# Down projection with its first two token pairs interleaved, part stores one block later, and row sums spread over blocks

## The chip, the cores and the metric

The kernel runs on one core of a Trainium2 chip. The metric is the device time of one launch in microseconds: before the change 2499.06 us, the median of three runs (2497.41 to 2502.0). The engines are named as in the profile: PE is TensorE (the matrix engine), PEld its weight loads, DVE VectorE, ACT ScalarE, POOL GpSimd, SP SyncE, which here only issues transfers.

## What is computed

One layer of a hybrid encoder for 17 tiles of 128 tokens (2048 tokens of a prompt, 8 x 16 of running streams), width 1024, hidden width 2816. Two mixers (a gated delta rule and a short gated convolution) come first; the change doesn't touch them. Then follows the feed-forward part:

```python
    mix = jnp.concatenate([o, sc_out.astype(x.dtype)], axis=-1) @ w_o
    x = x + rmsnorm(mix, norm_mix_post)

    h = rmsnorm(x, norm_ffn_pre)
    f = (jax.nn.silu(h @ w_gate) * (h @ w_up)) @ w_down
    x = x + rmsnorm(f, norm_ffn_post)
    return x, conv_new, S_new, sc_new
```

All is float32. The matrix engine gets each operand as two fp32r parts, a rounded one (made by a cast on ACT) and what the rounding left (made by a subtraction on DVE or POOL), and every product is three matmuls: high by high, high by low, low by high.

## The kernel before

**Blocks.** The large products of the feed-forward part are done by a scheme with seven products on 2x2 blocks instead of eight. Both operands are needed in seven combinations of blocks ("parts"), and the results are put together from the seven products.

**Gate and up** (`gate_up`, 1095 to 2018 us). Tokens go in three passes `gi` over groups of 6, 6 and 5 tiles; in each pass 22 blocks `f` of 128 hidden columns are done. A block is 84 matmuls (L1284) of 128x384, or 128x320 in the last pass: four products into four banks (`gu_start`), then three more onto three of these. Between the two, ACT copies the first sums out of the banks (`m1`, `m7`, `m5`, L1316 to L1318), and the later matmuls overwrite these banks. DVE combines the copies with the later sums, and ACT applies the SiLU (L1327, L1332). The product of gate and up is the hidden activation; DVE makes the activation parts for the down projection from it (tile `pt`, written in every other block), and the DMA queue of ACT stores them (`partd` L1356 and L1358, `lastd` L1350 for the fifth tile of the odd group). The stores stand at the end of the block in the text; they wait for DVE's sums in `pt`.

The first operand of the next pass is prepared while a pass runs: `hs` are loaded after blocks 4 to 11, and at block 16 (`f == NF - 6`) `ffn_sums` makes all row sums of that operand, three DVE operations for each of four `k`, twelve in one go (L1182 to L1185).

**Down** (`down_pair`, `down_single`, `down_chunk`, 2018 to 2485 us). The hidden width is cut into five chunks `ch` of 4, 4, 4, 4 and 6 blocks (`FCHUNKS`), so `c` is 2 in the first four and 3 in the last. In each chunk all pairs of token tiles are gone through: eight pairs and a `single`. A pair has seven products, each of `c` x 3 matmuls of 128x512 (L1450), from 7 activation parts and 7 x `c` weight parts. Activation parts are loaded from `partd` (`load_parts`, tile `ar`, three buffers) and split (`split`, L1431 ACT cast, L1434 subtraction on DVE or POOL). A weight part is made from raw weights (`dr`, four buffers) by a cast on ACT (L1132) and a subtraction on POOL, each third one on DVE (L1134); `prep_step` does one such step. A ring of `NDW` = 21 weight parts lies in four `dr`, one `sA`/`sB`, twelve `da` and four `dn` tiles. The sums leave the banks by DVE additions (L1409) into `acc`, or in chunk 0 by ACT copies. `fbank` hands out the eight PSUM banks in turn; a pair takes four.

In chunk 0 the first two activation parts of the first pair (`first_parts`) and five weight parts are made during pass 2 of gate and up (`f` = 4 and 11 to 15).

**The end of a pair.** In the last chunk `finish` squares the sum (ACT, L1459), makes the norm's factor (L1460, L141, POOL L143), multiplies with the gain (DVE L1463), adds the residual (DVE L1468) and stores both halves of the result, one by ACT's queue and one by SP's (L1470). `down_pair` ends with two more DVE subtractions there (L1509, L1510). The `single` comes last in the last chunk (`tail`), after the first pair in the others.

**What sets the order.** Each engine executes its instructions in order. That order comes from a scheduler that simulates the engines over the text of the kernel (`issue_after` gives it edges); the text's order is its priority. DMA issues stand in the order of the engine that issues them, so a transfer that waits for data holds back all later transfers of its queue.

Of the kernel before, what the change touches and what calls it, by code (L numbers as in the profile page):

```python
# [86 lines left out]
def kernel(  # L87
# [1010 lines left out]
    SUMS = ("sA", "sB", "sC", "sD")  # L1098

    def down_chunk(ch):  # L1100
# [11 lines left out]
        def part(i, q):  # L1112
# [12 lines left out]
            if m == NDR:  # L1125
                w = [ks.tile([P, 512], F32R, tag=nm, name=nm) for nm in SUMS[:2]]
            else:
                pool, b = (dr, NDR) if m < NDR else (da, NDQ) if m <= NDR + NDQ else (dn, NDW - NDR - 1 - NDQ)
                w = pool.tile([P, 2, 512], F32R, tag="dw", name="dw", bufs=b)
                w = [w[:, 0], w[:, 1]]  # L1130
# [30 lines left out]
    with ExitStack() as ph:  # L1161
# [14 lines left out]
        def ffn_sums(gi, hs, fs):  # L1176
            hw = len(FGROUPS[gi]) * P // 2
            t3, t2 = [], []
            for k in range(KH):
# [8 lines left out]
        def ffn_prep(gi, hs, sums=None, fs=None):  # L1188
# [3 lines left out]
            for nm in PARTS:  # L1192
                for k in range(KH):
                    b11, b12, b21, b22 = blocks(gi, hs, k)
                    if nm == "T3" and not sums:
                        t3.append(fs.tile([P, HW], F32, tag="t3", name="ft3", bufs=KH)[:, :hw])
# [36 lines left out]
        def gu_weights(gi, f):  # L1233
# [12 lines left out]
            else:  # L1246
                nc.sync.dma_start(out=rg, in_=w_gu[f, 0].rearrange("p k c -> p (k c)"))
                wl[:] = [nc.sync.dma_start(out=ru, in_=w_gu[f, 1].rearrange("p k c -> p (k c)"))]
                s = [(fe if q > 1 else ks).tile([P, 512], F32R, tag=nm, name=nm).bitcast(F32) for q, nm in enumerate(SUMS)]
# [55 lines left out]
        def gate_up(gi, f, X, banks):  # L1305
# [12 lines left out]
            A.copy(s5, b4)  # L1318
# [27 lines left out]
            if n % 2:  # L1346
                for vi, v in enumerate((v1, v2)):
                    nc.scalar.dma_start(out=lastd[ch][:, kk % 2, q, vi * 64:vi * 64 + 64], in_=v[:, hw - 64:hw])
            if kk % 2:
# [5 lines left out]
                for j in range(n // 2):  # L1355
                    nc.scalar.dma_start(out=partd[gi][ch][j, :, 1:7, q, :], in_=pt[:, :, j * P:(j + 1) * P])  # L1356
            else:
                nc.scalar.dma_start(out=partd[gi][ch][:, :, 0, q, :].rearrange("j p c -> p j c"),  # L1358
                                    in_=v1[:, :n // 2 * P].rearrange("p (j c) -> p j c", c=P))

        held, first_parts, gmark = {}, [], {}
        for gi in range(len(FGROUPS)):
            if gi:
                *_, hid = ffn_prep(gi, hs, t3)
            for f in range(NF):
# [7 lines left out]
                if gi + 1 < len(FGROUPS):  # L1373
# [3 lines left out]
                    if f == NF - 6:  # L1377
                        with tc.issue_after(gmark["V"].ins):
                            t3 = ffn_sums(gi + 1, hs, fd)
                elif f == 2:  # L1380
# [3 lines left out]
                    a = dr.tile([P, 2, c * P], F32, name="ar0")  # L1384
                    with tc.issue_after(wl[0].ins):
                        nc.sync.dma_start(out=a, in_=partd[0][0][0, :, 0:2].rearrange("p i q c -> p i (q c)"))
                    first_parts = [dr.tile([P, 2, c * P], F32R, name=f"as0{i}") for i in range(2)]
                elif f == 4:
                    with tc.issue_after(gmark["A"].ins), tc.issue_after(gmark["V"].ins):
                        for i, b in enumerate(first_parts):  # L1390
                            A.copy(b[:, 0], a[:, i])
                            V.tensor_sub(b[:, 1], a[:, i], b[:, 0].bitcast(F32))
                    dprep += [down_chunk(ch) for ch in dorder]
                    prep_step(1)
                elif f == 7:
                    prep_step(1)
                elif 11 <= f < 12 + NDR:
# [223 lines left out]
```

## Time and profile before

| | us |
|---|---|
| median of three runs | 2499.06 |
| lowest and highest | 2497.41, 2502.0 |
| profiled execution | 2499.33 |
| its span on the engines | 2497.4 |
| mixers, output projection | 0 to 1095 |
| gate and up, three passes | 1095 to 2018 |
| down, five chunks | 2018 to 2485 |
| tail | 2485 to 2497.4 |

The granted TensorE clock over the span is 0.996. Busy shares are of the whole span. In a row of the timeline the first two numbers are start and duration (of a group, from its first start to its last end), then engine, line, operation and count, and in brackets how long the engine had been idle before it and what ended that. A row by windows gives the stretch, its length, how much of it the engine was busy, the number of instructions, the granted clock, the share of the DMA engines and their rate. A row by line gives count, busy time and mean ns, idle time before it and what ended most of it; a row by tile gives count, shortest/median/longest ns and the first and last start. A row of waits says who waited for what, us in total, times, longest.

### The profile page before, as it was taken

Reading aid. Unit: us, or ns where it says so; the run is one execution under the profiler, and the core shown is the slowest. Engines: PE = TensorE matmul, PEld = TensorE weight load, DVE = VectorE, ACT = ScalarE, POOL = GpSimd, SP = SyncE. Lnnn points to the kernel's source line nnn. Section 1 sums busy time; section 2 is a strip of 40 time slices with the busy share of each in tenths; the row PEclk is TensorE's granted clock in tenths of the full one; section 3 lists DMA queues with packets and bytes.
Section 4 is the critical chain, followed back from the end, with each engine's and each line's share of the span. In section 5 each row is a group of like instructions: output and inputs, shape, how many; then the busy total and the mean of one; then the engine's idle time right before and its main releaser. Section 6 shows DMA issues by size and latency. Waiting matters only on the chain. (4 is left out here: it accounts for less than half of the span.)

```text
span 2497.4 us, 39376 instructions
## 1 busy us (share of the span) xinstructions
PE 2454.7 (98%) x14374; PEld 2246.4 (90%) x14374; DVE 1617.7 (65%) x3045; ACT 1051.4 (42%) x2337; POOL 579.4 (23%) x656
## 2 busy tenths in 40 slices
PE   8999999999999999999999999999999999999998
PEld 6888888999999988889999999999999987887786
DVE  5875754646656555878788844455555564677698
ACT  5546544545435343444443522224233345333343
POOL 1101001101011000146655300000000055455564
PEclk9999999999999999999999999999999999999999
DMA  7764556666766556688876888878898743343475
GB/s 248 260 221 150 196 202 209 241 229 228 252 225 239 206 177 225 199 307 300 290 266 238 289 261 274 263 240 268 293 303 284 252 147 123 93 127 125 131 223 185
DMA packets 281593, 561.38 MB, mean 225 GB/s; under 512 B 25332, under 2 KB 174136, under 8 KB 264120
## 3 DMA queue, kind: packets, MB, share of 16 engines
q1 hardware_dynamic: 161344, 483.51, 56.9%
q10 hardware_dynamic: 120056, 75.37, 9.7%
q8 instruction: 113, 1.85, 0.3%
q14 instruction: 80, 0.66, 0.1%
HBM read 400.09 MB, written 158.70 MB: 224 GB/s over the span
## 5 line engine op out<-in xcount | busy, mean ns | idle before, releaser
L1284 PE MATMUL fbank<-xh,fw 128*128 128x384 f32 (+1 forms) x3696 | 899.6, 326 | 5.3 <-ACT m L1316 2.5
L302 PE MATMUL dbank<-hi,w 128*128 128x384 f32 (+1 forms) x2240 | 665.6, 366 | 9.7 <-ACT w L281 6.4
L1284 PEld LDWEIGHTS fbank<-xh,fw 128*128 128x128 f32 x3696 | 652.3, 188 | 6.9 <-ACT m L1316 2.8
L1284 PE MATMUL fbank<-xl,fw 128*128 128x384 f32 (+1 forms) x1848 | 602.4, 326 | 0.0
L302 PEld LDWEIGHTS dbank<-hi,w 128*128 128x128 f32 x2240 | 414.4, 189 | 48.9 <-ACT w L281 6.4
L1450 PE MATMUL fbank<-dw,as 128*128 128x512 f32 x1884 | 442.7, 393 | 8.1 <-DVE as L1434 2.9
L1450 PEld LDWEIGHTS fbank<-dw,as 128*128 128x128 f32 x1884 | 353.2, 188 | 91.5 <-DVE acc L1409 4.3
L302 PE MATMUL dbank<-lo,w 128*128 128x384 f32 (+1 forms) x1120 | 401.3, 358 | 0.0
L1284 PEld LDWEIGHTS fbank<-xl,fw 128*128 128x128 f32 x1848 | 347.5, 188 | 0.0
L1434 POOL TENSOR_TENSOR as<-ar,as 128x256 fp32r<-128x256 f32 (+1 forms) x207 | 186.8, 912 | 225.5 <-ACT as L1431 222.6
L302 PEld LDWEIGHTS dbank<-lo,w 128*128 128x128 f32 x1120 | 211.8, 189 | 17.8 <-issue 1.0
L1409 DVE TENSOR_TENSOR acc<-acc,fbank 128x512 f32<-128x512 f32 x248 | 166.1, 681 | 93.7 <-PE fbank L1450 79.8
L1431 ACT CAST as<-ar 128x256 fp32r<-128x256 f32 (+1 forms) x288 | 118.3, 427 | 181.0 <-PE fbank L1450 134.1
L1134 POOL TENSOR_TENSOR dw<-dr,dw 128x512 fp32r<-128x512 f32 x48 | 69.8, 1465 | 522.8 <-ACT dw L1132 522.8
L1259 ACT CAST fw<-rg 128x512 fp32r<-128x512 f32 x124 | 77.3, 623 | 193.6 <-PE fbank L1284 169.5
L306 DVE SCALAR_TENSOR_TENSOR acc<-R,vec,acc 128x512 f32<-128x512 f32 (+2 forms) x180 | 121.4, 676 | 46.6 <-ACT acc L336 40.5
L1329 DVE TENSOR_TENSOR c<-u,fbank 128x384 f32<-128x384 f32 (+1 forms) x66 | 34.8, 528 | 113.0 <-PE fbank L1284 113.0
L1327 ACT ACTIVATE m<-fbank 128x384 f32<-128x384 f32 (+1 forms) x66 | 31.3, 474 | 127.5 <-PE fbank L1284 119.8
L1325 DVE TENSOR_TENSOR m<-m,m 128x384 f32<-128x384 f32 (+1 forms) x44 | 23.1, 525 | 87.6 <-ACT m L1318 87.5
L1260 POOL TENSOR_TENSOR fw<-rg,fw 128x512 fp32r<-128x512 f32 x44 | 70.5, 1603 | 33.6 <-ACT fw L1259 33.6
L328 POOL COPY hist<-R 128x3 f32<-128x3 f32 x60 | 18.9, 316 | 239.7 <-ACT R L311 194.1
L1318 ACT COPY m<-fbank 128x384 f32<-128x384 f32 (+1 forms) x66 | 30.5, 462 | 80.8 <-PE fbank L1284 64.7
(362 smaller groups left out, 3543.9 us busy)
## 6 DMA issues: line engine op xcount, KB each, us to landing
w<-wsplit SPq DMA_DIRECT2D x105, 1024.0 KB, 4.9
fw<-fsplit SPq DMA_DIRECT2D x188, 512.0 KB, 4.6
fsplit<-fw SPq DMA_DIRECT2D x94, 512.0 KB, 3.8
partd<-pt ACTq DMA_DIRECT2D x88, 384.0 KB, 6.4
rg<-in_w_gu SPq DMA_DIRECT2D x62, 512.0 KB, 4.0
wsplit<-w SPq DMA_DIRECT2D x28, 1024.0 KB, 4.9
ar<-partd SPq DMA_DIRECT2D x48, 384.0 KB, 3.3
wr<-in_w_in SPq DMA_DIRECT2D x34, 512.0 KB, 5.7
```

Of the source, the lines that this page charges most:

```text
L302: T.matmul(ps[:, :c], l[:, k, :], r[k][:, :c], start=(k == 0 and r is hi and l is wh), stop=(k == KD - 1 and l is wl))
L306: r = V.scalar_tensor_tensor(acc, raw(d), w[:, d:d + 1], acc, op0=ALU.mult, op1=ALU.add)
L1134: e.tensor_tensor(out=w[1], in0=v, in1=w[0].bitcast(F32), op=ALU.subtract)
L1259: A.copy(w[:, 0], v)
L1260: e.tensor_tensor(out=w[:, 1], in0=v, in1=w[:, 0].bitcast(F32), op=ALU.subtract)
L1284: T.matmul(ps, w_[:, c], b_[k][:, :hw], start=(first and k == 0 and ci == 0), stop=(k == KH - 1 and ci == 2), skip_group_check=not first)
L1327: A.activation(sg0, b1, AF.Silu)
L1329: V.tensor_add(c21, u2, b3)
L1409: V.tensor_add(dst, dst, ps)
L1431: ins = A.copy(a[:, 0, :n], v)
L1434: e.tensor_tensor(out=a[:, 1, :n], in0=v, in1=a[:, 0, :n].bitcast(F32), op=ALU.subtract)
L1450: T.matmul(ps, a[:, x_, q * P:(q + 1) * P], w[y_], start=(start and q == 0 and ci == 0), stop=(q == c - 1 and ci == 2), skip_group_check=True)
```

## The change

Six edits go together:

1. The stores of a block's parts are kept in a list (`fstores`) and issued by ACT's queue after the third copy (`m5`) of the next block. Those of the very last block go on SP.
2. The twelve row sums for the next pass are made three at a time behind blocks 12, 14, 16 and 18 (`SUMF`).
3. The tiles `sC` and `sD` move to the pool that lives on into down, so the ring of weight parts gets a second `s` tile and one `dn` tile less. The part made ahead from block 11 on now starts at block 10: six weight parts. A third activation part, part 0 of the second pair, is loaded after block 4 and split after block 7 of pass 2.
4. In each chunk the first two pairs are generators that are stepped in turn, one product each (in chunk 0 by a short table); `down_single` and the other pairs follow. Loads of parts 4 to 6 may come later than before.
5. `ar` tiles are filled without gaps. `accs` is two tiles, and in the tail the product with the gain goes to a tile of its own (`xm`), written while ACT squares.
6. Both halves of a result go by SP's queue, except in the tail and the held rows; the load of the gain stands at chunk 2 in the text.

```diff
@@ ring of weight parts
-            if m == NDR:
-                w = [ks.tile([P, 512], F32R, tag=nm, name=nm) for nm in SUMS[:2]]
+            if NDR <= m < NDR + 2:
+                w = [ks.tile([P, 512], F32R, tag=nm, name=nm) for nm in SUMS[2 * (m - NDR):2 * (m - NDR) + 2]]
...
@@ gate_up
-            A.copy(s5, b4)
+            ins = A.copy(s5, b4)
+            with tc.issue_after(ins.ins):
+                while fstores:
+                    nc.scalar.dma_start(**fstores.pop(0))
...
-                    nc.scalar.dma_start(out=partd[gi][ch][j, :, 1:7, q, :], in_=pt[:, :, j * P:(j + 1) * P])
+                    fstores.append(dict(out=partd[gi][ch][j, :, 1:7, q, :], in_=pt[:, :, j * P:(j + 1) * P]))
...
+            if gi + 1 == len(FGROUPS) and f + 1 == NF:
+                while fstores:
+                    nc.sync.dma_start(**fstores.pop(0))
@@ the passes
-                    if f == NF - 6:
+                    if f in SUMF:
                         with tc.issue_after(gmark["V"].ins):
-                            t3 = ffn_sums(gi + 1, hs, fd)
+                            t3 = ffn_sums(gi + 1, hs, fd, t3 if f > SUMF[0] else None, [SUMF.index(f)])
...
+                        nc.sync.dma_start(out=a[:, 0], in_=partd[0][0][1, :, 0].rearrange("p q c -> p (q c)"))
...
-                elif 11 <= f < 12 + NDR:
+                elif 10 <= f < 12 + NDR:
@@ finish
+            m = dr.tile([P, D], F32, tag="dr", name="xm", bufs=4).rearrange("p (h c) -> p h c", h=2) if tail else None
...
-                A.activation(junk, v[:, h], AF.Square, accum_out=ss[:, h:h + 1])
+                A.activation(junk, v[h], AF.Square, accum_out=ss[:, h:h + 1])
+                if tail:
+                    ins = V.tensor_mul(m[h], v[h], gpo[:, 512 * h:512 * h + 512])
...
-                    (nc.sync if h else nc.scalar).dma_start(out=yr[r0:r0 + n, c], in_=xt[p0:p0 + n, c])
+                    (nc.scalar if (tail or hold) and not h else nc.sync).dma_start(out=yr[r0:r0 + n, c], in_=xt[p0:p0 + n, c])
@@ down_pair
+            duo = pairs.index(u) < 2
+            ready = first_parts[:2] if (ch, u) == (0, pairs[0]) else first_parts[2:] if (ch, u) == (0, pairs[1]) else []
+            if duo:
+                parts = ready + load_parts(src, len(ready), 7 if len(ready) == 2 else 4)
+                yield
...
+                if duo:
+                    yield
@@ the loop over pairs
+            duo = [down_pair(ch, u, False) for u in pairs[:2]]
+            for i in (0, 1, 0, 0, 1, 1) + (0, 1) * 5 if not ch else (0, 1) * 8:
+                next(duo[i])
+            for d in duo:
+                next(d, None)
```

**ACT in the first pass of gate and up.** Rows are in ACT's order; `m` are the copies `m1`, `m7` and `m5` out of the banks, `fw` weight parts of later blocks, `partd` the stores. Before:

```order
L1316 COPY m_11609<-fbank 128x384
L1259 CAST fw<-ru 128x512
L1356 DMA partd_0_113<-pt 128x6x128 x3
L1317 COPY m_11610<-fbank 128x384
L1259 CAST fw<-sD 128x512
L1318 COPY m_11611<-fbank 128x384
L1259 CAST fw<-rg 128x512
```

And with the change:

```order
L1317 COPY m_11606<-fbank 128x384
L1260 CAST fw<-ru 128x512
L1318 COPY m_11607<-fbank 128x384
L1260 CAST fw<-sD 128x512
L1319 COPY m_11608<-fbank 128x384
L1322 DMA partd_0_113<-pt 128x6x128 x3
L1260 CAST fw<-rg 128x512
```

The three stores stood between the first and the second copy, and stand behind the third now.

**SP between gate/up and down.** `fw<-fsplit` are the last weight parts of gate and up, `ar` the first activation loads of down, `lastd` and `partd_4` the stores of the last block. Before:

```order
L1257 DMA fw<-fsplit_154 128x1024 x4
L1440 DMA ar<-partd_0_113 128x2x256
L1440 DMA ar<-partd_0_113 128x3x256
L1440 DMA ar<-lastd_128 128x2x256
L1440 DMA ar<-partd_0_113 128x2x256
```

And with the change:

```order
L1258 DMA fw<-fsplit_154 128x1024 x4
L1366 DMA lastd_132<-pt 128x64
L1455 DMA ar<-partd_0_113 128x1280
L1455 DMA ar<-partd_0_113 128x768 x2
L1366 DMA lastd_132<-pt 128x64
L1366 DMA partd_4_127<-pt 128x6x128 x2
L1455 DMA ar<-lastd_128 128x512
```

A store of the last block stands ahead of the first loads now; the first loads are larger (parts 2 to 6 of the first pair, then parts 1 to 3 and 4 to 6 of the second).

**PE at the start of down.** `as00` and `as01` are the activation parts made ahead for the first pair, `as02` the one for the second, `dw` and `sA`/`sB` weight parts. Before:

```order
L1450 MATMUL fbank_20754<-dw_19392,as00_18161 128x512 x3
L1450 MATMUL fbank_20754<-dw_19528,as00_18161 128x512 x3
L1450 MATMUL fbank_20755<-dw_19669,as01_18162 128x512 x3
L1450 MATMUL fbank_20755<-dw_19806,as01_18162 128x512 x3
L1450 MATMUL fbank_20756<-sA_19947,as_20772 128x512
```

And with the change:

```order
L1465 MATMUL fbank_20764<-dw_19257,as00_18158 128x512 x3
L1465 MATMUL fbank_20764<-dw_19396,as00_18158 128x512 x3
L1465 MATMUL fbank_20765<-dw_19534,as01_18159 128x512 x3
L1465 MATMUL fbank_20765<-dw_19674,as01_18159 128x512 x3
L1465 MATMUL fbank_20785<-dw_19257,as02_18160 128x512 x3
L1465 MATMUL fbank_20785<-dw_19396,as02_18160 128x512 x3
L1465 MATMUL fbank_20786<-dw_19534,as_20796 128x512 x2
```

Six more matmuls on parts that are made ahead follow the first twelve, with the same two weight parts as the first six.

83 lines of the change are left out of this document (50 added, 33 removed).

## The prediction

> **What bounds the kernel now.** I read the busy times of the page first, then the windows of TensorE over the two stages that the change touches, then the timeline at every window that holds too few matmuls.
>
> ```profile
> PE 2454.7 (98%) x14374; PEld 2246.4 (90%) x14374; DVE 1617.7 (65%) x3045; ACT 1051.4 (42%) x2337; POOL 579.4 (23%) x656
> ```
>
> TensorE is busy 98% of the span. The change removes no matmul, so it can win only where TensorE stands still or runs at half clock. Busy time hides part of that (a matmul that waits in the pipe counts as busy), so I count matmuls in windows instead.
>
> ```profile
> core 0: us, PE busy (x), PEclk, DMA share, GB/s
> 1136.00:1148.00 12.00, 10.69 (x62) 1.00 0.82 275
> 1164.00:1180.00 16.00, 15.03 (x87) 1.00 0.90 308
> 1200.00:1240.00 40.00, 40.00 (x232) 1.00 0.87 296
> 1366.00:1390.00 24.00, 21.20 (x112) 0.93 0.71 249
> 2018.00:2042.00 24.00, 20.59 (x78) 0.93 0.61 205
> 2026.00:2034.00 8.00, 5.42 (x17) 0.79 0.49 155
> 2050.00:2090.00 40.00, 40.00 (x175) 1.00 0.34 103
> 2108.00:2124.00 16.00, 14.88 (x65) 1.00 0.58 189
> 2192.00:2208.00 16.00, 15.53 (x67) 1.00 0.51 174
> 2276.00:2296.00 20.00, 19.21 (x82) 1.00 0.42 141
> 2358.00:2374.00 16.00, 14.32 (x62) 1.00 0.60 217
> ```
>
> An undisturbed gate/up window holds 232 matmuls in 40 us (0.172 us each), an undisturbed down window 175 (0.229 us each). Against these rates, the gate/up windows 1136, 1164 and 1366 lack 7.6, 5.8 and 27.2 matmuls: 1.3 + 1.0 + 4.7 = **7.0 us**. The window after the start of down (2018 to 2042) lacks 27: **6.2 us**. The windows at the four chunk changes (2108, 2192, 2276, 2358) lack 5, 3, 5.5 and 8: 21.5 x 0.229 = 4.9 us. In all 18.1 us can be won there; the rest of both stages runs at its matmul rate.
>
> **Gate/up: stores and row sums.** What ends the waits there:
>
> ```profile
> 1136.66 2.04 ACTq L1356 DMA_DIRECT2D partd<-pt  x3
> 1138.80 0.48 ACT L1317 COPY m<-fbank 128x384 f32<-128x384 f32 x1 [4.69 <-PE fbank L1284]
> 1139.33 0.44 PE L1284 MATMUL fbank<-xh,fw 128*128 128x384 f32 x1 [1.31 <-ACT m L1317]
> 1373.33 0.52 ACT L1332 ACTIVATE c<-c 128x384 f32<-128x384 f32 x1 [9.24 <-DVE c L1331]
> 1374.27 0.44 PE L1284 MATMUL fbank<-xh,fw 128*128 128x384 f32 x1 [2.52 <-ACT m L1316]
> L1182 DVE TENSOR_TENSOR ft<-fh 128x384 f32<-128x384 f32 x4 | 5.0, 1301 | 0.0
> L1185 DVE TENSOR_TENSOR ft<-fh 128x384 f32<-128x384 f32 x4 | 2.0, 546 | 0.0
> ```
>
> At 1136.66 ACT's queue sits in the stores of the block before until 1138.70, because they wait for DVE's sums; the copy out of the bank (L1317, at 1138.80) stands behind them, and the matmul that overwrites that bank's sum starts at 1139.33. The order after the change puts these stores behind the third copy of the next block. What is then late is only the landing in memory, which no one needs for whole passes, and the reuse of the one buffer pt a block later, for which DVE would wait. A block is 84 matmuls, 14.5 us, and pt is next written almost two blocks after its first use, so even a store issued a block late has several us; I cost it at nothing, and if that cover failed it would cost the wait again, 1.0 to 1.3 us a block where it occurs. I credit 1.3 + 1.0 us.
>
> At 1373.33 ACT had waited 9.24 us for DVE, which was in the burst of row sums: four of 1301 ns, eight of 546 or so, over 9 us. ACT's copies of the next block are in order behind it, so TensorE stopped 2.52 us, and the clock fell to 0.93 over the window. Spread out, a block gets 1.3 + 2 x 0.55 = 2.4 us of DVE in place of 9.6. DVE is busy 65% of the span, so a block of 14.5 us has some 5 us free; 2.4 fits. I credit 4.7 us; the bounds are 4.7 and, if the loss goes by DVE's time wherever it is spent (four blocks with a quarter each), nothing.
>
> Six weight parts instead of five and a third activation part are made during pass 2: one more load of 128 KB, one cast and one subtraction, and one part earlier. In that pass the trace has no wait of TensorE, and ACT (42% busy) and DVE have room: nothing. Sum of gate/up: **-7.0 us** (bounds -2.3 and -7.0).
>
> **The start of down.**
>
> ```profile
> 2006.58 2.13 SPq L1440 DMA_DIRECT2D ar<-partd  x2
> 2016.86 0.49 DVE L1344 TENSOR_TENSOR pt<-c,m 128x320 f32<-128x320 f32 x1
> 2017.82 2.94 PE L1450 MATMUL fbank<-dw,as 128*128 128x512 f32 x12
> 2029.02 1.19 PE L1450 MATMUL fbank<-dw,as 128*128 128x512 f32 x4 [2.58 <-DVE as L1434]
> ar<-partd SPq DMA_DIRECT2D x4, 384.0 KB, 3.2
> w<-wsplit SPq DMA_DIRECT2D x105, 1024.0 KB, 4.9
> L1431 ACT CAST as<-ar x15: 401/405/411, 2019.9 to 2042.9; 128x256 fp32r<-128x256 f32 x15
> L1434 DVE TENSOR_TENSOR as<-ar,as x6: 410/924/1509, 2022.1 to 2044.5; 128x256 fp32r<-128x256 f32 x6
> L1134 POOL TENSOR_TENSOR dw<-dr,dw 128x512 fp32r<-128x512 f32 x48 | 69.8, 1465 | 522.8 <-ACT dw L1132 522.8
> ```
>
> Now 12 matmuls stand ready at 2017.82; after them each product waits for a weight part (POOL takes 1.47 us for one, while six matmuls take 1.37) or a split activation (a median of 0.92 on DVE). With two pairs interleaved each weight part feeds 12 matmuls, 2.7 us, and 18 stand ready: 18 x 0.229 = 4.1 us, to 2021.9. That is the gain.
>
> Against it stands SP's order. The three loads of activations are now issued from 2006.58 on, eleven us early. In the new order a store of lastd that waits for pt (L1344, done at 2017.35) stands ahead of them. So the loads leave from about 2017.7 on, one every 0.4 us or so (an estimate from the two issues of the first row, which take 2.13 us with their waits). The first two are 640 and 384 KB, together 1 MB. By the row for 384 KB the second lands 3.2 us after its issue, at 2021.3; by that for 1 MB both need 4.9 us, to 2022.6. Then come a cast (0.41) and a subtraction (0.41 at best): ready at 2022.1 to 2023.4. TensorE runs dry at 2021.9, so it stands 0.2 to 1.5 us. I take the later one, because the loads share the engines with the last block's stores, and add 0.8 for restarts while the first splits and weights line up (the three short waits of 0.2 to 0.4 us that the start has now): 2.3 us are left of 6.2. Gain **-3.9 us**, bounds -6.0 and 0.
>
> Here a rule can be weighed. A stop of 2.58 us (before 2029.02) lies in a window whose clock is 0.79 and which holds 17 matmuls instead of 35: the lost 18 are 4.1 us, 1.5 more than the stop. So a stop of that length costs over half as much again. The Trainium skill ("TensorE: Matmul & The Clock Gate", "Part 1: The HAM clock gate") says that the clock falls only after an idle window of about 3.4 us that runs freely; by it a stop of 2.3 us could never cost more than itself. The trace differs at 2.52 and at 2.58 us, so the measurement decides. By the rule this term would be the same -3.9, and the case below that turns on the clock would give about 1.5 us less.
>
> **The chunk changes.**
>
> ```profile
> 2112.61 1.14 ACT L1132 CAST dw<-dr 128x512 fp32r<-128x512 f32 x2 [1.72 <-DMA dr<-in_w_dn]
> 2116.32 0.96 PE L1450 MATMUL fbank<-dw,as 128*128 128x512 f32 x3 [1.01 <-DVE acc L1409]
> ```
>
> ACT stands in order at a weight cast whose raw tile has not landed; the activation casts and DVE's sums out of the banks queue behind it, and TensorE waits for a bank. In the interleaved part a weight is needed half as often, and a bank is used again after eight products instead of four (11 us instead of 5.5). That would absorb a lateness of 1.7 us entirely. But the second pair's parts 4 to 6 are now loaded behind four loads of raw weights on SP, so I leave about 0.7 us at each change but the smallest: 2.1 of 4.9 stays. **-2.8 us**, bounds -4.9 and 0.
>
> **The last chunk and the tail.**
>
> ```profile
> core 0: us, DVE busy (x), PEclk, DMA share, GB/s
> 2382.00:2485.00 103.00, 96.11 (x162) 1.00 0.69 215
> L1468 DVE SCALAR_TENSOR_TENSOR xr<-acc,f2r,xr 128x512 f32<-128x512 f32 x29 | 28.7, 1027 | 0.5
> L1463 DVE TENSOR_TENSOR acc<-acc,gpo 128x512 f32<-128x512 f32 x31 | 21.7, 702 | 4.0 <-ACT junkd L1459 4.0
> L1509 DVE TENSOR_TENSOR acc<-acc 128x512 f32<-128x512 f32 x7 | 6.2, 881 | 0.2
> L1510 DVE TENSOR_TENSOR acc<-acc 128x512 f32<-128x512 f32 x8 | 6.0, 753 | 0.2
> 2488.89 0.16 DVE L1460 TENSOR_TENSOR fss<-fss 128x1 f32<-128x1 f32 x1
> 2490.23 0.15 DVE L141 TENSOR_SCALAR f3m<-fss 128x1 f32<-128x1 f32 x1
> ```
>
> Here DVE is nearly as full as TensorE: 96.1 of 103 us. The interleaving lets both first pairs end together, so the work that closes pair 0 is done a pair later: 4 x 0.70 + 4 x 1.03 + 0.88 + 0.75 = 8.5 us of DVE. DVE has 6.9 us free in the rest of the stage, so by the end it can be 1.6 us behind, and the last sums are late by that; banks give slack of several products before TensorE itself waits. I take +1.6 with 0.8 for the moments where it piles up: **+2.4 us** (bounds 0 and 8.5). In the tail, f3m waits 1.2 us (2489.05 to 2490.23) behind a product and a sum that the new text takes from its way, by writing the product to a tile of its own: **-1.2 us** (bounds -1.7, with a wait less on the split accumulator, and 0).
>
> **Sum**, against the profiled execution of 2499.33 us (0.27 above the median of the runs): -7.0 - 3.9 - 2.8 + 2.4 - 1.2 = -12.5, so **2486.8 us**.
>
> **The rivals.** *Only gate/up pays*: TensorE gets its ready matmuls at the start of down, but the loads behind lastd, the weights and DVE's heap take all of it back: 2499.3 - 7.0 = 2492.3. For it speaks that every term of down rests on one queue, SP, which the change fills in another order; against it, that the need for weights truly halves. *The clock at the start*: the first loads are late by more than 2.5 us beyond the ready work, the stop costs 4.1 us as before 2034, and the short waits stay: the 3.9 are gone, 2490.7. It decides from a landing at 2023.6, a microsecond later than I take. *DVE's heap*: pair 0's 8.5 us come in one piece and TensorE waits for banks, +6 more than taken: 2493. *Slower*: SP in the last chunk.
>
> ```profile
> SPq L1470 <- DVE xr L1468: 36.8, 12, 6.0
> ```
>
> SP already waits 36.8 us in 12 results' stores for DVE. The change puts both halves of each result on SP, in order ahead of the next pairs' loads. Where DVE is a pair behind, a store holds back a load until later than it is needed: landing 3.2, cast 0.4 and subtraction 0.9, 4.5 us before its matmul. If each of the six pairs after the interleaved ones stops TensorE for that, 27 us come on top, 2514. It decides once DVE is later than the lead with which the loads are issued, about a pair's work (63 matmuls, 14.4 us). Against it: DVE's lag by the sum above is 8.5 us at most, and shrinks. *The change does not do what it says*: the order shows the interleaving and the moved stores, and only the first loads lie other than the words suggest; that is in the sum.
>
> **How the numbers follow.** The forecast has a chance of 0.56, gate/up alone 0.13, the clock 0.12, DVE's heap 0.08, the slower case 0.08, and 0.03 is for what I have not seen. A measurement of this kernel tells 0.2%, 5 us, from no change, so faster means under 2494.1. Nearly all of the first four cases lie there, but gate/up alone and the heap only by 1 to 2 us, so part of their 0.21 goes to no change: faster 0.80, the same 0.12, slower 0.08. Downward the range reaches to where all that was counted is won: 18.1 + 1.2 = 19.3, 2480, and a little lower, 2478, for short waits that no window shows; upward it takes in the cases that give most of the down stage back, and a loss at DVE's upper bound: 2497.
>
> **What would show it.** Windows 1130 to 1390 without a gap, and ACT's copies not behind a store: the gate/up term. Three loads issued near 2011 (all times 7.0 earlier) and TensorE's first wait some 4 us after its first down matmul, under 2 us long and with full clock: the start. Chunk changes lacking 1 to 3 matmuls each. In the last chunk TensorE waiting for DVE's sums by not more than 2 to 3 us in all, and f3m right behind its sum. It would be wrong if the row sums still delayed ACT, if SP's wait at lastd grew, or if SP's stores of results stood ahead of late loads.

## The result and the profile after

The changed kernel takes 2492.43 us, the median of 22 runs (2487.77 to 2499.07), against 2499.75 us for the kernel before in 22 runs (2496.26 to 2506.93). The ratio is 0.9973, with a 95% interval of 0.9966 to 0.9979: 7.3 us faster, where 12.5 were forecast. The profiled execution of the changed kernel, 2497.51 us, was one of its slower ones.

TensorE's busy time of the span, in the page of the changed kernel, doesn't show a gain at all:

```profile
PE 2458.0 (98%) x14374; PEld 2249.2 (90%) x14374; DVE 1616.9 (65%) x3050; ACT 1049.6 (42%) x2337; POOL 583.9 (23%) x651
```

The reason lies ahead of the change. Two windows of the mixers, TensorE's row, first of the kernel before:

```profile
0.00:100.00 100.00, 90.41 (x425) 1.00 0.73 260
700.00:800.00 100.00, 98.44 (x616) 1.00 0.71 240
```

And of the changed kernel:

```profile
0.00:100.00 100.00, 91.86 (x418) 0.97 0.72 257
700.00:800.00 100.00, 96.62 (x594) 0.98 0.69 234
```

The same matmuls in the same order, yet 7 and 22 fewer in the same stretch. Between these two executions the mixers differ by 4.2 us, and in the further runs below, none of which touches them, they ended anywhere between 1093.9 and 1099.4 us. So spans can't be compared to within the effects sought. What can is the time from the first matmul of a stage to the first of the next, read from each trace (chunks: after each 360 matmuls of down; the last chunk to the start of its last matmul, the tail from there; us):

| run | pass 0 | pass 1 | pass 2 | chunk 0 | 1 | 2 | 3 | 4 | tail |
|---|---|---|---|---|---|---|---|---|---|
| before | 330.8 | 320.3 | 271.0 | 89.1 | 84.2 | 82.7 | 84.3 | 126.9 | 12.5 |
| changed | 324.1 | 322.0 | 271.0 | 87.7 | 83.5 | 82.9 | 84.3 | 126.2 | 14.1 |

Gate and up win 5.1 us, down 2.6, and the tail loses 1.7: 6.0 us in this pair of executions, close to the 7.3 of the medians.

One pair of executions doesn't settle terms this small. In the runs below many stages are left with the same instructions in the same order as in the changed kernel, and still differ: gate and up took 914.6 to 917.3 us and once 921.4 (nine executions, median 915.6), chunk 0 86.6 to 87.7 (five), chunks 1 to 3 in sum 250.7 to 251.9 (seven), chunk 4 126.1 to 127.3 (five), the tail 13.5 to 14.2 (seven). In the order of the kernel before, three executions each, chunks 1 to 3 took 251.2 to 251.4, chunk 4 126.7 to 127.8 and the tail 12.5 to 13.0; for its gate and up there is one execution alone.

The windows of TensorE in the changed kernel that answer to those shown of before:

```profile
core 0: us, PE busy (x), PEclk, DMA share, GB/s
1135.00:1147.00 12.00, 12.00 (x72) 1.00 0.98 352
1378.00:1392.00 14.00, 13.29 (x77) 1.00 0.83 286
1430.00:1442.00 12.00, 10.83 (x62) 1.00 0.62 186
2017.00:2041.00 24.00, 22.22 (x92) 0.93 0.64 211
2050.00:2058.00 8.00, 7.16 (x30) 1.00 0.37 111
2119.00:2131.00 12.00, 11.70 (x50) 1.00 0.40 122
2200.00:2210.00 10.00, 9.84 (x40) 1.00 0.24 74
2282.00:2292.00 10.00, 9.29 (x39) 1.00 0.26 78
2438.00:2446.00 8.00, 6.92 (x29) 1.00 0.88 291
```

At the undisturbed rates (5.8 matmuls a microsecond in gate/up, 4.375 in down) the first window is full now. The others lack 4, 8, 13, 5, 2.5, 4, 5 and 6 matmuls. New among them: the one at 1430, where pass 1 begins, and the one at 2438, in the last chunk. And the chunk changes no longer stop at the change, but 14 to 21 us behind it.

### The profile page after: what moved, and what is told of

Its sections match the earlier page's. It is cut to its first block, busy times and chain, and to the rows that moved or that the text cites. A ratio compares the mean times of both kernels' runs of the same rounds, so it can differ in the third digit from the quotient of the medians.

```text
span 2495.7 us, 39308 instructions
## 1 busy us (share of the span) xinstructions
PE 2458.0 (98%) x14374; PEld 2249.2 (90%) x14374; DVE 1616.9 (65%) x3050; ACT 1049.6 (42%) x2337; POOL 583.9 (23%) x651
## 4 chain that ended last, share of the span: by engine, by line
PE 79%; DVE 6%; DMA 2%; issue 2%; POOL 2%; ACT 1%; ACTq 0%; DVEq 0%; SPq 0%; POOLq 0%
PE fbank L1285 33%; PE dbank L302 21%; PE fbank L1465 11%; PE dbank L1050 4%; PE tbank L1050 4%; POOL dw L1135 1%; DVE xr L1488 1%; DVE acc L1423 1%; PE tbank L347 1%; PE gbank L757 1%; PE obank L702 1%; POOL as L1448 1%; PE ftbank L1079 1%; PE obank L724 1%; PE gbank L716 1%
## 5 line engine op out<-in xcount | busy, mean ns | idle before, releaser
L1465 PE MATMUL fbank<-dw,as 128*128 128x512 f32 x1782 | 421.0, 392 | 3.7 <-ACT as L1445 1.8
L1465 PEld LDWEIGHTS fbank<-dw,as 128*128 128x128 f32 x1782 | 333.6, 188 | 82.3 <-ACT as L1445 3.6
L1336 ACT ACTIVATE c<-c 128x384 f32<-128x384 f32 (+1 forms) x66 | 33.4, 507 | 101.8 <-DVE c L1335 101.8
L1261 POOL TENSOR_TENSOR fw<-rg,fw 128x512 fp32r<-128x512 f32 x44 | 64.6, 1468 | 45.3 <-ACT fw L1260 45.3
```

The source lines that it names most:

```text
L1261: e.tensor_tensor(out=w[:, 1], in0=v, in1=w[:, 0].bitcast(F32), op=ALU.subtract)
L1465: T.matmul(ps, a[:, x_, q * P:(q + 1) * P], w[y_], start=(start and q == 0 and ci == 0), stop=(q == c - 1 and ci == 2), skip_group_check=True)
```

## Experiments

**The late stores alone**, on the kernel before:

```diff
+            ins = A.copy(s5, b4)
+            with tc.issue_after(ins.ins):
+                while fstores:
+                    nc.scalar.dma_start(**fstores.pop(0))
```

> The kernel before with the late stores alone. Theory (the stores ahead of the bank copies on ACT were what stopped TensorE): the three waits near 1139, 1172 and 1380 us go, 1.58 + 1.25 + 0.56 us, so pass 0 of gate and up takes 327.4 us instead of 330.8; the burst of row sums near 1374 still costs its 4.3 us. On SP the store of the last block stands ahead of the first loads of down, with only 12 matmuls ready there, so chunk 0 gets longer, by some 3 us (89.1 to about 92). Sum about -0.4 us. Rival (TensorE's waits there were not due to the stores): pass 0 stays at 330.8. Rival for SP's order (loads there have time in hand): chunk 0 stays at 89.1 and the sum is -3.4.

Pass 0 fell to 324.0, by 6.9 us, not 3.4: the stop near 1374 is gone too, though the burst of row sums is still there. Pass 1 rose to 324.1, by 3.8. Chunk 0 took 89.6, only 0.5 more. The time was 2498.62 against 2499.93 (ratio 0.9993, 0.9984 to 1.0002): more than half of what the stores win in pass 0 comes back in pass 1.

**The spread row sums alone**, on the kernel before:

```diff
-                    if f == NF - 6:
+                    if f in SUMF:
```

> The kernel before with the row sums spread over blocks 12, 14, 16 and 18 alone. Theory (the burst is the cause of the stop at 1374, and its spreading leaves a rest): pass 0 loses the 4.3 us at 1374 and gets one wait of about 1 us behind block 18 or 19, as the changed kernel has near 1388: 330.8 to 327.5; pass 1 gets the 1.6 us that the changed kernel has at the change of pass (its first block), 320.3 to 322.0. Rival (the new wait at the change of pass comes from another edit): pass 1 stays at 320.3. Rival (the rest near 1388 comes from the late stores, not from the sums): pass 0 falls to 326.5. Chunk 0 and all behind it as before.

Pass 0 took 330.0 (0.8 less), pass 1 320.3: the rival for pass 1 holds, and no theory foresaw pass 0. The stop of 4.9 us became three of 1.3 to 1.6, one behind each of three sets of sums. The timeline of this run at the first of them shows ACT as the prediction showed it for 1139:

```profile
1343.93 1.17 ACTq L1357 DMA_DIRECT2D partd<-pt  x1
1345.67 0.47 ACT L1319 COPY m<-fbank 128x384 f32<-128x384 f32 x1
1346.19 0.44 PE L1285 MATMUL fbank<-xh,fw 128*128 128x384 f32 x1 [1.41 <-ACT m L1319]
```

The sums make DVE late with pt, the store on ACT waits for pt, and the copy waits behind the store. Sums and stores were one mechanism, and the stores carry it: with them alone moved, the stop goes though the burst stays. The whole was 2502.02 (1.0010, 1.0000 to 1.0019).

**What stops TensorE at the start of pass 1.** The timeline of the changed kernel there:

```profile
1404.12 2.27 ACTq L1322 DMA_DIRECT2D partd<-pt  x3
1405.15 19.37 SPq L1258 DMA_DIRECT2D fw<-fsplit  x12
1418.25 0.56 DVE L1356 TENSOR_TENSOR pt<-a,a 128x384 f32<-128x384 f32 x1 [6.01 <-DMA partd<-pt]
1435.21 0.48 ACT L1319 COPY m<-fbank 128x384 f32<-128x384 f32 x1 [1.89 <-DVE pt L1348]
1435.74 0.44 PE L1285 MATMUL fbank<-xh,fw 128*128 128x384 f32 x1 [1.17 <-ACT m L1319]
```

Three stores leave ACT's queue by 1406.4, a block later than they used to, and together with twelve loads of 512 KB on SP. DVE wants to write pt again for the last block of the pass and stands 6.01 us until they have landed, at 1418.25, twelve us after their issue. Behind that write stands its whole preparation of pass 1, and TensorE has to wait in block 0 of that pass. Over the stage, the rows of DVE's waits (us in total, times, longest) are, for the kernel before, for the late stores alone, and for the changed kernel:

```profile
DVE pt L1352 <- DMA partd<-pt: 6.4, 3, 2.5
```

```profile
DVE pt L1355 <- DMA partd<-pt: 28.2, 10, 7.7
```

```profile
DVE pt L1356 <- DMA partd<-pt: 24.0, 8, 8.3
```

Eight other runs below have this part of the program in the same order. DVE's wait at that place, and the time that TensorE loses in block 0 of pass 1, were 3.76 and 0.22 us, 4.53 and 0.77, 5.19 and 0.85, 5.23 and 0.89, 5.25 and 0.90, 5.64 and 1.30, 5.78 and 1.42, 6.01 and 1.66 (the rows above), and 10.23 and 5.84. From 5.19 us on, the one is the other less 4.3 to 4.4 us; the two shortest waits cost more than that. (At the shortest and the longest the profile puts DVE's wait down to a load of SP, not to the stores.) To take the wait away, the first write of pt in a block, which needs nothing of that block and therefore stood at its head, was moved behind the block's last product:

```diff
-                V.tensor_sub(pt[:, 1, :hw], a11, a21)
+                with tc.issue_after(gmark["V"].ins):
+                    V.tensor_sub(pt[:, 1, :hw], a11, a21)
```

> The changed kernel with one of DVE's four sums of a block moved: the one that writes pt from the block before alone (pt row 1), which the order puts at the head of DVE's work of the block, comes behind the product that ends gate times up. Theory (a store issued a block later lands later, DVE waits for it at this first write of pt, 24 to 36 us in all, and what waits there at the last block of pass 0 pushes DVE's preparation of the next pass behind, which stops TensorE 336 us into the stage): DVE's waits for the landing of partd fall below 8 us, the stop of 0.8 to 1.6 us at 336 goes, pass 1 takes 320.3 us as before the change, gate and up in sum 643.5 to 644.5 instead of 644.3 to 646.3. Rival (DVE is late at the change of pass by its own work, not by the waits): the stop at 336 stays above 0.7 us, pass 1 at 321 or more.

The trace of this run has no wait of DVE for partd left, pass 1 takes 320.3 us, and the window at its start is full (TensorE's row):

```profile
1420.00:1440.00 20.00, 20.00 (x118) 1.00 0.84 259
```

Pass 1 took 320.3 in the run with all four edits too, and 320.5 to 326.2 in the nine executions without the move. Gate and up take 915.3 in all three passes, without the 271.0 of pass 2 644.3, as expected, but this total lies within the spread of the changed kernel's order. The time was 2492.67, ratio 0.9962 (0.9950 to 0.9975), and can't be told from the changed kernel's.

**The start of down.** The timeline of the changed kernel bears out the order on SP: the store that waits for pt, then the three loads, the casts 5.6 us later, and TensorE dry after its 18 matmuls:

```profile
2016.57 0.32 SPq L1366 DMA_DIRECT2D lastd<-pt  x1
2016.98 1.35 SPq L1455 DMA_DIRECT2D ar<-partd  x3
2017.01 4.29 PE L1465 MATMUL fbank<-dw,as 128*128 128x512 f32 x18
2022.62 1.33 ACT L1445 CAST as<-ar 128x256 fp32r<-128x256 f32 x4 [4.42 <-DMA ar<-partd]
2023.08 0.73 PE L1465 MATMUL fbank<-dw,as 128*128 128x512 f32 x2 [1.78 <-ACT as L1445]
```

> The changed kernel with the stores of the very last block on ACT's queue instead of SP's, so that nothing stands ahead of the first three loads of down on SP. Theory (SP's store waiting for pt delays the loads; that makes the stop of 1.94 us and the half clock behind it): the loads leave some ten us earlier, the stop and the 1.8 us of half clock go, chunk 0 falls from 87.7 to about 84 us, the whole by 3.7. Rival (ACT, which now waits for pt with the activation casts behind it, delays them as much): the stop stays at 1 us or more and chunk 0 falls by less than 1.5 us.

Chunk 0 took 86.0 us, 1.7 less than in the execution shown above; against the 86.6 to 87.7 of the five executions it is 0.6 to 1.7 less, well short of 3.7, and the rival's 1.5 isn't excluded. The stop, 1.1 to 1.8 us in those five, shrank to 0.5 us; ACT's casts now stand behind the stores on ACT:

```profile
2009.39 4.29 PE L1465 MATMUL fbank<-dw,as 128*128 128x512 f32 x18
2013.74 1.33 ACT L1445 CAST as<-ar 128x256 fp32r<-128x256 f32 x4 [3.15 <-issue]
2014.20 0.74 PE L1465 MATMUL fbank<-dw,as 128*128 128x512 f32 x2 [0.51 <-ACT as L1445]
```

TensorE's loss some 35 us into down, where it waits for sums and copies out of the banks, was 1.9 us, against 1.4 in the execution above and 1.8 to 2.4 in the four others with the stores on SP, so it isn't a price of this edit. The time, 2494.63 (0.9981, 0.9969 to 0.9994), can't be told from the changed kernel's. What the clock cost there was asked of the run with another tail, whose instructions have the same order up to there. Windows of TensorE from 4 us after the first down matmul, changed kernel:

```profile
2021.00:2025.00 4.00, 2.22 (x8) 0.87 1.01 331
2025.00:2029.00 4.00, 4.00 (x14) 0.70 0.48 160
```

And the run with another tail:

```profile
2015.80:2019.80 4.00, 2.27 (x11) 1.00 1.04 343
2019.80:2023.80 4.00, 4.00 (x19) 1.00 0.49 157
```

With the same stop (1.78 and 1.73 us), the clock fell in one execution and not in the other, and chunk 0 took 87.7 us in both: the loss 35 us in was 2.4 instead of 1.4 us. That doesn't make the clock free. In the run with another tail a subtraction of DVE ahead of the awaited sum took 1.78 us where it took 0.68 in the changed kernel. The run with the moved write of pt had neither, and chunk 0 took 87.0 after a stop of 1.65 us; its window 8 to 12 us behind the first down matmul:

```profile
2018.70:2022.70 4.00, 4.00 (x20) 1.00 0.51 165
```

By this pair the slow stretch cost at most 0.7 us.

**The interleaving.** In the changed kernel:

```diff
-            for i in (0, 1, 0, 0, 1, 1) + (0, 1) * 5 if not ch else (0, 1) * 8:
+            for i in (0,) * 8 + (1,) * 8:
```

> The changed kernel with the first two pairs of each chunk one after the other again, all else as changed. Theory (the interleaving moves the lack of weight parts from a chunk's start to the end of the two pairs, where DVE and POOL are full, and wins little): chunks 1 to 3 take 251.2 us in sum as before, against 250.7 changed; chunk 0 some 89.6, as with the late stores alone, against 87.7; chunk 4 126.9 against 126.2: 3 us more in all. Rival (the step of the prediction: the need for weights and banks is halved for good, 2.8 us at the chunk changes and 3.9 at the start of down): chunks 1 to 3 rise by 2.5 us or more, chunk 0 to 91.5 or more, 6 to 7 us in all.

Chunk 0 took 87.3, within the 86.6 to 87.7 that it takes with interleaving; chunks 1 to 3 took 260.2 against 250.7, chunk 4 130.0 against 126.2. (Pass 1 was 4.2 longer by the wait of 10.23 us above, which this execution happened to have.) The time was 2506.81, ratio 1.0024 (1.0012 to 1.0036). Both theories miss: at the start of down the interleaving is worth nothing, at the chunk changes far more than 2.8 us. TensorE in the first 20 us of chunks 1 and 3, first without, then with it:

```profile
2104.00:2124.00 20.00, 16.64 (x69) 0.98 0.41 148
2277.00:2297.00 20.00, 17.78 (x69) 0.91 0.42 160
```

```profile
2104.70:2124.70 20.00, 19.90 (x87) 1.00 0.41 142
2271.10:2291.10 20.00, 19.29 (x82) 1.00 0.40 142
```

But the kernel before had no interleaving either, and took 251.2 us for these chunks. It had the `single` between the first two pairs, and the change moves it behind the second. The next run has the pairs one after the other and the `single` between them:

> The changed kernel with the first two pairs one after the other, as in the run without interleaving, but with the single again between them, as before the change (in chunks 0 to 3). That run took 260.2 us for chunks 1 to 3 where the kernel before takes 251.2 and the changed one 250.7. Theory (the single's 24 matmuls, which need four weight parts that are ready, stretched the need for weights in the kernel before just as the interleaving does in the changed one, and the interleaving replaces what the moved single takes away): chunks 1 to 3 fall to 251 to 254 us, chunk 4, which has no single there, stays near 130. Rival (the loads that the change puts off or joins make the plain order slow): they stay above 257.

Chunks 1 to 3 took 251.3 us in sum, chunk 4 130.0, and chunk 0 93.2. So in chunks 1 to 3 of the kernel before, the `single` did what the interleaving does: it gave TensorE 24 matmuls on weight parts that were there. The edit takes that away and puts its own in place. Chunk 0 is another matter: there the `single` between the pairs cost 5.9 us against the run without it. TensorE waited 0.92 us for a cast of ACT and 1.53 for a sum of DVE 28 to 32 us in, and the clock fell to 0.50 behind that. The time was 2502.49 (1.0010, 0.9996 to 1.0023).

**What the chunk changes wait for.** The windows of DVE and POOL 10 to 20 us behind the change to chunk 1, first DVE and then POOL of the changed kernel, and last DVE of the kernel before:

```profile
2115.00:2125.00 10.00, 10.00 (x15) 1.00 0.09 28
```

```profile
2115.00:2125.00 10.00, 9.87 (x8) 1.00 0.09 28
```

```profile
2117.00:2127.00 10.00, 10.00 (x15) 1.00 0.22 66
```

DVE is full there in both, and POOL beside it in the changed one. TensorE's waits of the changed kernel end on either of the two (its rows in chunks 1 and 3):

```profile
2126.15 1.66 PE L1465 MATMUL fbank<-dw,as 128*128 128x512 f32 x6 [0.20 <-DVE acc L1423]
2285.69 2.41 PE L1465 MATMUL fbank<-dw,as 128*128 128x512 f32 x8 [0.69 <-POOL as L1448]
```

One run, executed once, takes work from DVE; it leaves out sums that the result needs:

```diff
             b11, b12, b21, b22 = raw[q]
-            if i == 1:
+            if 0 < ch < len(FCHUNKS) - 1:
+                pass
+            elif i == 1:
```

> The changed kernel without DVE's sums of raw weight blocks in chunks 1 to 3 (eight of 0.7 to 1.2 us a chunk; the weight parts there are made from single blocks), all else as changed. Theory (in the first 20 us of a chunk DVE, and POOL beside it, is full with making weight parts, and the interleaving only moves that lack to the end of the two pairs): chunks 1 to 3 lose their waits of 0.9, 1.2 and 1.5 us almost entirely and take 82.0 to 82.9 us each, 248 in sum instead of 250.7. Rival (the loads of the second pair's last parts, behind the loads of raw weights on SP, are late): the sum stays above 250.

Chunks 1 to 3 took 82.4, 81.6 and 83.9 (there a wait of 0.82 us for a sum of DVE stayed), 248.0 in sum, where the seven executions with these sums took 250.7 to 251.9. Over the change to chunk 1 TensorE has no gap any more (its row):

```profile
2085.00:2125.00 40.00, 40.00 (x176) 1.00 0.41 130
```

Loads behind other loads are not the cause there, since the order of the loads is unchanged. Whether DVE's time or the chain of sum, cast and subtraction behind each weight part was the limit, this run doesn't tell apart.

**The last chunk.** Without interleaving in chunk 4 alone:

> The changed kernel without the interleaving in the last chunk alone. Theory of the prediction (both pairs end together, so DVE gets their closing work in one heap, 2.4 us): chunk 4 falls from 126.2 to about 123.8 us. Rival (the heap is absorbed, and the interleaving wins about what it costs): chunk 4 stays within 0.7 us of 126.2, near the 126.9 of the kernel before. Chunks 0 to 3 don't change.

Chunk 4 rose to 131.1; the time was 2497.18 (0.9990, 0.9978 to 1.0002). Both ideas miss: against the 126.1 to 127.3 of the five executions the interleaving is worth 3.8 to 5.0 us there, heap included, given the other edits. Why the plain order takes 130 to 131 with them and 126.9 without, the runs don't settle; no `single` stood early in this chunk in either kernel.

**SP's stores of results**, with the first half of every result on ACT again:

> The changed kernel with the first half of every result on ACT's queue again, as before the change. If SP's stores of results, waiting for DVE ahead of the loads, cost time in the last chunk, chunk 4 gets shorter by 1 us or more. Theory: the loads have a pair's time in hand, so chunk 4 stays within 0.5 us of 126.2, or gets longer, since ACT then waits for DVE ahead of its activation casts.

Chunk 4 took 125.7, 0.5 less than in the changed kernel's profiled execution and 0.4 to 1.6 less than in the five; it took 125.8 in the run with all four edits. The tail took 13.0, against 13.5 to 14.2: DVE came to the last sums 0.7 us earlier after the last matmul. So this order can be worth more than the theory's 0.5; a loss of 27 us, as the prediction's rival has it, there wasn't. The time was 2492.10 (0.9965, 0.9953 to 0.9977).

**The tail.** The timeline of the changed kernel:

```profile
2483.89 0.69 DVE L1478 TENSOR_TENSOR xm<-accs,gpo 128x512 f32<-128x512 f32 x1
2484.50 0.74 DVE L1488 SCALAR_TENSOR_TENSOR xr<-acc,f2r,xr 128x512 f32<-128x512 f32 x1
2485.16 0.68 DVE L1423 TENSOR_TENSOR accs<-accs,fbank 128x512 f32<-128x512 f32 x1
2485.94 0.63 ACT L1476 ACTIVATE junkd<-accs 128x512 bf16<-128x512 f32 x1 [4.86 <-DVE accs L1423]
2487.64 0.15 DVE L141 TENSOR_SCALAR f3m<-fss 128x1 f32<-128x1 f32 x1
```

The product with the gain no longer waits for the squares, so the scheduler put it, and a residual of the last pair behind it, ahead of the second sum, which ACT's first square needs. ACT was idle for 4.86 us, and f3m comes 6.0 us after the last matmul's start, where it came after 5.3 before.

```diff
-            for h in range(2):
-                A.activation(junk, v[h], AF.Square, accum_out=ss[:, h:h + 1])
-                if tail:
+            for h in (1, 0) if tail else (0, 1):
+                sq = A.activation(junk, v[h], AF.Square, accum_out=ss[:, h:h + 1])
+            for h in (1, 0) if tail else ():
+                with tc.issue_after(sq.ins):
                     ins = V.tensor_mul(m[h], v[h], gpo[:, 512 * h:512 * h + 512])
```

> The changed kernel with another order in the tail: ACT squares the half of the last sum that is ready first (half 1) ahead of half 0, and the products with the gain come behind the squares in the order. Theory (in the changed kernel ACT waits for half 0, whose sum stands on DVE behind a product and a residual of another tile): from the last matmul to the norm's factor 0.85 us less, tail 14.1 to 13.3 us, nothing else moves. Rival (the end is set by the landing of stores that are under way anyway): the tail stays at 14.1.

The tail took 13.2, f3m came after 5.1 us. (In the run with ACT's queue f3m came after 5.3 us, with DVE's order in the tail left as in the timeline above, so DVE's lag from the last pairs is the other part of this delay.) The time was 2493.55 (0.9969, 0.9959 to 0.9978). Together with the last block's stores on ACT:

> The changed kernel with the last block's stores on ACT and the reordered tail together. Theory (the two are independent): chunk 0 some 86.0 us instead of 87.7, tail 13.2 instead of 14.1, all else as in the changed kernel: 2.6 us less in the stages. Rival (the stop that goes in chunk 0 comes back in the chunks behind it): chunks 0 to 4 in sum as changed, 464.6, and only the tail's 0.9 stays.

Chunk 0 took 86.3 and the tail 12.7, but chunks 0 to 4 in sum 465.3, 0.7 more than in the changed kernel's profiled execution. That is what the rival says, but it doesn't show it: with the same order, chunks 1 to 4 took 376.9 to 379.0 us in five executions, this one at the upper end. The time was 2492.25 (0.9965, 0.9952 to 0.9977).

**Four edits together:**

> The changed kernel with the late sum of pt, the last block's stores on ACT, the first halves of results on ACT and the reordered tail together. If these are independent: gate and up 643.5 to 644.5, chunk 0 86.0, chunks 1 to 3 and 4 as changed (250.7 and 126), tail 12.6 to 13.2; against the changed kernel 3.5 to 5 us less in the stages. Rival (what is won at one place comes back at the next): the sum from the first matmul of gate and up to the end stays within 1.5 us of the changed kernel's.

Gate and up took 914.4, the tail 12.0 (f3m after 4.3 us), but down 465.5: against the changed kernel's profiled execution, chunk 0 gave 0.9 and chunk 1, 85.1 us where the others took 83.5 to 84.3, took 1.7 back. From the first matmul of gate and up to the end 1391.9 us against 1395.8. The time was 2490.44 us, ratio to the kernel before 0.9952 (0.9940 to 0.9965), the lowest of all but the run without raw sums. Its interval and the changed kernel's, 0.9966 to 0.9979, only just don't overlap.

## Why the prediction was right, and where it wasn't

The direction and the range held; the gain was 7.3 us of 12.5. The measured 2492.43 is nearer to the rival *only gate/up pays* (2492.3, chance 0.13) than to the forecast, though it is no pure case of it: the start of down keeps 1.5 to 2.5 us, and the tail loses about as much. Term by term, from the stage table, TensorE's missing matmuls and the spread of the stages:

- **Gate and up, -7.0: measured -5.1** in this pair, -6.5 by the median of the nine executions. The three stops went. The step that failed is "What is then late is only the landing in memory, ... and the reuse of the one buffer pt a block later ... I cost it at nothing". The reuse was not free: DVE waited 24 us for it in place of 6.4, at the change of pass this cost TensorE 1.7 us, and the moved write removed exactly that. Another 0.7 us went at 1388, just behind the last set of row sums, in this execution; the runs don't show why. The attribution was wrong as well: the stop at 1374 went with the late stores alone, while the spread sums alone gave 0.8 us. Whether the spreading wins something beside the late stores stays open: pass 1 took 324.1 without it and 320.5 to 322.0 in eight executions with it, but 326.2 in one.
- **The start of down, -3.9: measured -1.5** in this pair, -1.5 to -2.5 over five executions. The stop came as forecast, 1.8 us, from the store ahead of the loads. The mis-sized part is what stands behind it: a slow stretch of the clock, and 1.4 us of waits some 35 us in, that the sum had as done with. That the interleaving brings the gain there is refuted: chunk 0 took 87.3 us without it. Which other part of the change does, stays open. In chunk 0 the kernel also puts every subtraction of the second pair on DVE, which the list of edits leaves out (13 activation subtractions on DVE from 2017 to 2060, where the kernel before has 9); no run tells what that costs.
- **The chunk changes, -2.8.** The last change lost its stop, the other three kept 0.6 to 1.1 us each. The prediction left 0.7 at the first, third and last change and nothing at the second. Chunks 1 to 3 won nothing that stands out of the spread, 250.7 to 251.9 us against 251.2 to 251.4. The step that failed is that a halved need takes the stop away: the waits come 14 to 21 us behind the change instead, for DVE and POOL, and in the windows shown DVE is as full there as before. Halving the need for a part does not make fewer parts.
- **The last chunk, +2.4**: TensorE lacks 6 matmuls, 1.4 us, at 2438, where the timeline has it waiting for a sum of DVE; the run without the interleaving in this chunk has no such wait there. The heap exists, and its size was too large by 1. What the term lacks is the other side: without the interleaving chunk 4 takes 3.8 to 5.0 us more.
- **Both together, -0.4**: chunks 1 to 4 took 378.1 us on average over five executions, and 378.5 over three of the order of before. That the sum of the two terms fits is luck; both were too large, with opposite signs.
- **The tail, -1.2: measured +1.7.** The wait for the product was taken away, and the scheduler filled the place with other work ahead of what mattered: f3m came 0.8 us later, and another order of the same work brought it 0.9 us forward. The other 0.9 is the landing of the last stores, 5.2 us against 4.3, and is in part chance: it varied from 4.6 to 5.2 in seven executions with this tail and from 4.3 to 4.8 in three with that of before.

The rival on SP's stores of results did not occur at its size: with ACT's queue chunk 4 was 0.4 to 1.6 us shorter, not 27. The clock rival was half right: the clock fell in the profiled execution, but at a cost of at most 0.7 us.

## What to carry to other kernels

A store that is issued later lands later, and the next write of its buffer waits: look where the first write of that buffer stands in its engine's order, and move that one write, before paying for a second buffer. When a stop goes from the start of a stretch, ask what the full engine behind it has to do in the whole stretch; if that is the same, the stop comes back at the stretch's end. And compare stage by stage, from traces, when an untouched stage varies by more than the effect, and take several executions: here a stage with the same instructions in the same order still varied by about 1 us, and gate and up by more.

## What the runs showed of the hardware

The second of the three row sums took 546 ns in the burst of the kernel before and 1651 ns spread out in the changed one, the same operation on the same sizes (the groups by line between 1300 and 1450 us, first of before, then of the changed kernel):

```profile
L1183 DVE TENSOR_TENSOR fh<-fh 128x384 f32<-128x384 f32 x4 | 2.0, 546 | 0.0
```

```profile
L1184 DVE TENSOR_TENSOR fh<-fh 128x384 f32<-128x384 f32 x4 | 6.6, 1651 | 0.0
```

Being spread out is not what makes it slow: the first row sum took 1301 ns in the burst too. In the burst POOL was idle for 6.45 us while the second sums ran. The timeline of the changed kernel shows one of them beside POOL:

```profile
1389.06 1.72 POOL L1261 TENSOR_TENSOR fw<-ru,fw 128x512 fp32r<-128x512 f32 x1 [3.60 <-ACT fw L1260]
1389.54 1.65 DVE L1184 TENSOR_TENSOR fh<-fh 128x384 f32<-128x384 f32 x1
```

DVE's subtraction begins at 1389.54, inside POOL's, and ends at 1391.19, 0.41 us after POOL's end at 1390.78. The Trainium skill ("SBUF — State Buffer", "SBUF: two separate sides") states that a DVE operation with two SBUF inputs and a GpSimd operation that reads SBUF hold a port pair as an exclusive lock, and that whoever comes second stands until the first is done. This trace agrees: 0.41 us is about what is left of a subtraction of 546 ns. A sum of pt whose record begins at 1389.07, ten ns behind POOL's, took only 0.55 us, so the starts of the records alone don't tell who came first. The prediction had put these sums at 2.4 us a block; a set took 3.5 us in the changed kernel (551, 1651 and 1256 ns).

The clock fell to 0.70 over 4 us behind a stop of 1.78 us in one execution, and stayed at 1.00 in others with stops of 1.73 and 2.02 us. The Trainium skill ("TensorE: Matmul & The Clock Gate", "Part 1: The HAM clock gate") says that the window runs freely, so that its phase decides, which fits; that it takes a whole idle window of about 3.4 us does not fit.
